# Block copies of the up-projection issued from SyncE's queue behind a semaphore, instead of from ScalarE's queue

## The chip, the cores and the metric

The kernel runs on one core of a Trainium2 chip. The metric is the device time of one execution in microseconds (us). A core has five engines, each with an instruction stream of its own that it works off in order: TensorE (PE in the profile), VectorE (DVE), ScalarE (ACT), GpSimd (POOL) and SyncE (SP). Engines wait for each other through semaphores, and an instruction that waits holds back all that stand behind it in its stream. A transfer (DMA) is issued by an instruction in one of these streams and then runs beside them.

## What is computed

Two layers of a bidirectional encoder over 1024 tokens of width 1024. The parts that matter here:

```python
def block_attention(q, k, v, scale):      # two groups of 6 heads in each layer
        s = jnp.einsum('bqhgd,bkhd->bhgqk', qi, k, preferred_element_type=jnp.float32) * scale
        p = jax.nn.softmax(s, axis=-1).astype(v.dtype)
        return jnp.einsum('bhgqk,bkhe->bqhge', p, v)
...
def conv_gated_ffn(h, w_up, conv_w, conv_b, w_down):
    a = h @ w_up
```

After the two attention groups come an output projection (`w_out`), a cross-attention to 256 memory tokens, and the gated FFN, whose product with `w_up` is done with seven block products instead of eight (the blocks are numbered m = 1 to 7). For four of the seven (m = 5, 6, 7, 3) sums of blocks of `w_up` are needed.

## The kernel before, in words

**Attention.** `attention()` walks over 24 items in each layer (12 heads, two halves of 512 queries), four steps `g` to an item. A step issues, in this order of the code: the scores of 128 queries (`score`: PE writes a `pair`, a PSUM tile of 128x1024, of which there are two; DVE takes the row maximum, line 292), the scaling of the step before (`scale`: a reciprocal on DVE, line 301, and a multiplication on POOL, line 302), two groups of four transposes of the item before (`turn`: PE line 137 into a `bank`, a PSUM tile of 128x512, of which there are four), the exponential (`expo`: ACT line 296), the products with the values (`value`: PE lines 315 and 316, one step late), and some side work (`fill`). Each transposed bank is split in two parts by `split`: ACT copies the high part (line 120, or 123 with a scale), then DVE subtracts it for the low part (line 121, or 124). Only when DVE has done so is the bank free for another group of transposes.

**Block sums.** During the attention the sums of `w_up` blocks are made by transfers from device memory to device memory: `up_copy` copies a piece (up to 1 MB), and four items later `up_add`, issued by POOL (line 781), adds another piece onto it. In each layer there are 24 copies and 24 additions. `extra` says at which item each is issued; all are issued in the step with `s == 2`. The sums are read in the FFN, after the attention.

**Order.** The code is not written to be run in this order word for word: the framework (`tile`) sorts each engine's stream by itself, by its own idea of what is ready when, and keeps only data dependences and what is pinned. `tc.keep_in_program_order` pins an instruction behind the one last written for the same engine. So a change in one stream can change the order in others.

**SP's queue.** SP issues the loads. During the attention it issued none between the loads of `w_uq` and `w_ukv` ahead of it and the eight loads of `w_out` towards its end (line 103, in `load`); POOL makes the high part of a loaded weight (line 107) and DVE the low part (line 108). Lines 693 and 694 (`y_split`) are a split of a finished output, done on POOL and DVE.

Of the kernel before, what the change touches and what calls it, by code (L numbers as in the profile page):

```python
# [11 lines left out]
ALU = mybir.AluOpType  # L12
# [57 lines left out]
def trunk(ctx: ExitStack, tc: tile.TileContext, a: dict, out: bass.AP):  # L70
    nc = tc.nc
# [8 lines left out]

    def f(ap):
        return ap.bitcast(F32) if ap.dtype == F32R else ap

    def stat():
        return stats.tile([P, 16], F32, tag="stat", name="stat")
# [14 lines left out]
    def load(src, cols, act=False):  # L100

        raw, hi, lo = sl.get(F32), sl.get(), sl.get()
        nc.sync.dma_start(raw[:, :cols], src)
        if act:
            nc.scalar.activation(hi[:, :cols], raw[:, :cols], AF.Copy)
        else:
            nc.gpsimd.tensor_scalar(hi[:, :cols], raw[:, :cols], 1.0, 0.0, ALU.mult, ALU.add)  # L107
        nc.vector.tensor_tensor(lo[:, :cols], raw[:, :cols], f(hi[:, :cols]), ALU.subtract)  # L108
        sl.put(raw)
        return hi, lo  # L110
# [6 lines left out]
    def split(src, hi, lo, scale=None):  # L117

        if scale is None:
            nc.scalar.activation(hi, src, AF.Copy)  # L120
            nc.vector.tensor_tensor(lo, src, f(hi), ALU.subtract)  # L121
        else:
            nc.scalar.activation(hi, src, AF.Copy, scale=scale)
            nc.vector.scalar_tensor_tensor(lo, src, scale, f(hi), ALU.mult, ALU.subtract)  # L124
# [115 lines left out]
    def head_norm(z, gain, tab):  # L240
# [29 lines left out]
        def turned():  # L270
# [3 lines left out]
            sl.put(*st["q"])  # L274

        return sums, scale, products, turned

    class Item:
# [20 lines left out]
        def scale(self, t):  # L299
            p, r = self.ps[t], stat()  # L300
            nc.vector.reciprocal(r[:, 0:1], self.den[:, t : t + 1])  # L301
            nc.gpsimd.tensor_scalar(p, p, r[:, 0:1], 0.0, ALU.mult, ALU.add)  # L302

        def turn(self, k):
            b = transpose4([p[:, k * P : (k + 1) * P] for p in self.ps])
# [85 lines left out]
    def layer(l, nt, last):  # L391
# [145 lines left out]
        for t in range(NT):  # L537
            b = proj(t, w_a, 416, 2)
            c, tt = divmod(t, TPC)
# [16 lines left out]
            if tt == TPC - 1:  # L556
                v, r = stat(), stat()
# [214 lines left out]
        up_sum = {(m, i): dpool.tile([P, n * CH + 16], F32, tag=f"u{l}_{m}_{i}", name=f"u{l}_{m}_{i}")[:, : n * CH] for m in (5, 6, 7, 3) for i, n in enumerate(UP_PARTS)}  # L772

        def up_piece(b, i):
            return a["w_up"][l, b][:, up_at[i] * CH : (up_at[i] + UP_PARTS[i]) * CH]

        def up_copy(m, i):
            tc.keep_in_program_order(nc.scalar.dma_start(up_sum[m, i], up_piece({5: 2, 6: 0, 7: 0, 3: 1}[m], i)))

        def up_add(m, i):  # L780
            tc.keep_in_program_order(nc.gpsimd.dma_start(up_sum[m, i], {5: lambda: up_piece(3, i), 6: lambda: up_sum[5, i], 7: lambda: up_piece(2, i), 3: lambda: up_sum[6, i]}[m](), accum_op=ALU.add))
# [61 lines left out]
        for n, (m, i) in enumerate(up_steps):  # L843
            extra.setdefault(n * 5 // 6, []).append(lambda m=m, i=i: up_copy(m, i))
            extra.setdefault(n * 5 // 6 + 4, []).append(lambda m=m, i=i: up_add(m, i))
# [537 lines left out]
```

## Time and profile before

| what | value |
|---|---|
| device time, median of 3 runs | 2869.32 us (2869.23 to 2872.6) |
| device time of the profiled execution | 2875.77 us |
| its span in the trace | 2873.6 us |
| PE busy | 97% of the span |
| DVE busy | 69% |
| ACT busy | 47% |
| POOL busy | 23% |

The busy shares are means over stages that differ: in the attention of the two layers (about 160 to 530 us and 1545 to 1960 us) DVE and ACT are far busier than in the FFN. An engine's idle time matters where the engine is the one that all wait for, here PE.

### The profile page before, as it was taken

How to read it: one execution, taken by the hardware profiler on the slowest of the kernel's cores; microseconds unless marked ns; L12 is line 12 of the kernel's file. 1: busy time of each engine (PE TensorE's matmuls, PEld its weight loads, DVE VectorE, ACT ScalarE, POOL GpSimd, SP SyncE). 2: the span in 40 equal slices, each digit the busy share in tenths (PEclk: the TensorE clock that was granted, in tenths of full speed). 3: DMA queues.
4: the chain of work that ended last, by engine and by line, in shares of the span. 5: the costliest groups of instructions: out<-in, count | busy, mean ns of one | idle time of the engine just before them, and what ended most of it. 6: DMA issues, size and time to landing. Idle time of an engine off the chain costs nothing. (4 is left out here: it accounts for less than half of the span.)

```text
span 2873.6 us, 37125 instructions
## 1 busy us (share of the span) xinstructions
PE 2798.3 (97%) x13909; PEld 2344.1 (82%) x13909; DVE 1975.6 (69%) x2825; ACT 1341.3 (47%) x2572; POOL 660.9 (23%) x628
## 2 busy tenths in 40 slices
PE   9998999999999999999999989999999999999998
PEld 7987787788878888888889777878887888888887
DVE  5578888656687777864445788895667877778544
ACT  4377877224554444310133778772345544443101
POOL 3244566320000000210123345663200000002100
PEclk9999999999999999999999999999999999999999
DMA  4015676311133333531110157752221333335311
GB/s 145 23 51 131 170 176 133 88 61 64 45 110 132 122 121 131 183 133 51 38 46 23 60 135 178 175 130 66 68 65 45 125 122 122 131 126 189 110 59 59
DMA packets 93635, 297.61 MB, mean 104 GB/s; under 512 B 10384, under 2 KB 11024, under 8 KB 83216
## 3 DMA queue, kind: packets, MB, share of 16 engines
q1 hardware_dynamic: 79488, 202.70, 21.1%
q0 software_dynamic: 6912, 46.14, 8.8%
q10 hardware_dynamic: 7056, 46.40, 4.5%
q8 instruction: 110, 1.80, 0.2%
q14 instruction: 69, 0.57, 0.1%
HBM read 267.94 MB, written 119.54 MB: 135 GB/s over the span
## 5 line engine op out<-in xcount | busy, mean ns | idle before, releaser
L113 PE MATMUL bank<-s,s 128*128 128x512 f32 (+4 forms) x1831 | 678.8, 371 | 5.9 <-DVE s L124 2.6
L115 PE MATMUL bank<-s,s 128*128 128x512 f32 (+4 forms) x1831 | 676.1, 369 | 0.9 <-DVE s L124 0.5
L114 PE MATMUL bank<-s,s 128*128 128x512 f32 (+4 forms) x1831 | 674.3, 368 | 0.0
L107 POOL TENSOR_SCALAR s<-s 128x1024 fp32r<-128x1024 f32 (+1 forms) x114 | 142.8, 1257 | 1374.3 <-DMA s<-in_w_down 1007.7
L121 DVE TENSOR_TENSOR s<-bank,s 128x512 fp32r<-128x512 f32 (+3 forms) x552 | 332.7, 631 | 109.1 <-ACT s L120 106.8
L120 ACT ACTIVATE s<-bank 128x512 fp32r<-128x512 f32 (+3 forms) x552 | 288.3, 555 | 238.4 <-PE bank L137 165.8
L113 PEld LDWEIGHTS bank<-s,s 128*128 128x128 f32 x1831 | 345.5, 189 | 62.7 <-DVE s L121 3.7
L115 PEld LDWEIGHTS bank<-s,s 128*128 128x128 f32 x1831 | 346.2, 189 | 53.8 <-DVE s L124 1.6
L114 PEld LDWEIGHTS bank<-s,s 128*128 128x128 f32 x1831 | 346.3, 189 | 50.9
L137 PE MATMUL bank<-ident,s 128*128 128x128 f32 (+1 forms) x2320 | 327.8, 276 | 45.5 <-DVE s L121 37.0
L137 PEld LDWEIGHTS bank<-ident,s 128*128 128x128 f32 (+1 forms) x2320 | 271.6, 141 | 108.0 <-issue 32.6
L302 POOL TENSOR_SCALAR s<-s,stat 128x1024 f32<-128x1024 f32 x192 | 224.5, 1169 | 249.1 <-DVE stat L301 159.6
L366 DVE TENSOR_TENSOR x<-x,bank 128x512 f32<-128x512 f32 x214 | 145.6, 683 | 195.5 <-PE bank L115 195.1
L292 DVE TENSOR_REDUCE stat<-pair 128x1 f32<-128x1024 f32 x192 | 234.2, 1220 | 65.4 <-PE pair L734 38.0
L1105 PE MATMUL bank<-s,s 128*128 128x512 f32 x704 | 274.8, 390 | 0.9 <-DVE s L206 0.9
L1106 PE MATMUL bank<-s,s 128*128 128x512 f32 x704 | 274.2, 389 | 0.0
L1104 PE MATMUL bank<-s,s 128*128 128x512 f32 x704 | 274.0, 390 | 0.0
L1057 ACT ACTIVATE s<-s 128x512 fp32r<-128x512 f32 x308 | 187.9, 627 | 161.7 <-PE bank L1106 49.8
L108 DVE TENSOR_TENSOR s<-s,s 128x1024 fp32r<-128x1024 f32 (+4 forms) x172 | 217.4, 1274 | 59.8 <-POOL s L107 46.1
L296 ACT ACTIVATE s<-pair,stat 128x1024 f32<-128x1024 f32 x192 | 214.3, 1116 | 16.9 <-DVE stat L292 10.3
L1058 DVE TENSOR_TENSOR s<-s,s 128x512 fp32r<-128x512 f32 x308 | 201.3, 687 | 24.4 <-ACT s L1057 20.8
L1104 PE MATMUL pair<-s,s 128*128 128x512 f32 x528 | 208.5, 395 | 1.2 <-ACT s L208 1.0
(164 smaller groups left out, 4519.5 us busy)
## 6 DMA issues: line engine op xcount, KB each, us to landing
s<-u SPq DMA_DIRECT2D x176, 256.0 KB, 3.0
u<-in_w_up ACTq DMA_DIRECT2D x40, 1024.0 KB, 6.5
s<-in_w_up SPq DMA_DIRECT2D x132, 256.0 KB, 3.3
g<-s SPq DMA_DIRECT2D x44, 512.0 KB, 2.8
s<-in_w_down SPq DMA_DIRECT2D x44, 512.0 KB, 4.4
s<-g SPq DMA_DIRECT2D x44, 512.0 KB, 5.4
u<-in_w_up POOLq DMA_DIRECT2D x20, 1024.0 KB, 9.8
u<-u POOLq DMA_DIRECT2D x20, 1024.0 KB, 10.0
```

The lines of the kernel that those rows point to most:

```text
L108: nc.vector.tensor_tensor(lo[:, :cols], raw[:, :cols], f(hi[:, :cols]), ALU.subtract)
L113: nc.tensor.matmul(o, l[0], r[0], start=first, stop=False)
L114: nc.tensor.matmul(o, l[0], r[1], start=False, stop=False)
L115: nc.tensor.matmul(o, l[1], r[0], start=False, stop=last)
L120: nc.scalar.activation(hi, src, AF.Copy)
L121: nc.vector.tensor_tensor(lo, src, f(hi), ALU.subtract)
L137: nc.tensor.transpose(b[:m, j * P : (j + 1) * P], s, ident)
L292: nc.vector.reduce_max(self.nm[:, 0:1], s, axis=AX.X, negate=True)
L302: nc.gpsimd.tensor_scalar(p, p, r[:, 0:1], 0.0, ALU.mult, ALU.add)
L1104: nc.tensor.matmul(o, lh, rh, start=k == 0 and m in (1, 5, 6), stop=False, skip_group_check=True)
L1105: nc.tensor.matmul(o, lh, rl, start=False, stop=False, skip_group_check=True)
L1106: nc.tensor.matmul(o, ll, rh, start=False, stop=k == 3, skip_group_check=True)
```

## The change

The copies are issued by SP instead of ACT, and are no longer pinned. Each waits by a semaphore for the POOL scaling (line 302) that was last written in the code when the copy is; `Item.last` remembers it. In a step with `s == 2` that is the scaling of the same item's second step.

```diff
@@ -80,6 +80,9 @@
+    def ins_of(i):
+        return getattr(i, 'ins', i)
...
@@ -299,7 +302,7 @@
         def scale(self, t):
             p, r = self.ps[t], stat()
             nc.vector.reciprocal(r[:, 0:1], self.den[:, t : t + 1])
-            nc.gpsimd.tensor_scalar(p, p, r[:, 0:1], 0.0, ALU.mult, ALU.add)
+            Item.last = nc.gpsimd.tensor_scalar(p, p, r[:, 0:1], 0.0, ALU.mult, ALU.add)
...
@@ -775,7 +778,8 @@
         def up_copy(m, i):
-            tc.keep_in_program_order(nc.scalar.dma_start(up_sum[m, i], up_piece({5: 2, 6: 0, 7: 0, 3: 1}[m], i)))
+            c = nc.sync.dma_start(up_sum[m, i], up_piece({5: 2, 6: 0, 7: 0, 3: 1}[m], i))
+            tc.add_manual_dep(ins_of(c), ins_of(Item.last).name, mybir.DependencyInfo(mybir.DependencyClass.Sync, mybir.DependencyReason.DATA), reason="not sooner")
```

No other instruction is added or taken away. Outside the attention the streams of PE, DVE, ACT and POOL stand in the same order as before; within it all four are sorted anew in places. In the rows that follow, line numbers of the changed kernel are 3 higher than those of the kernel before (L295 is L292, L304 is L301, L124 is L121, L106 is L103), and the copies are its line 781.

On DVE, at the turn from the fourth to the fifth item of the first layer (`s_187`, `s_188` are the two parts of transposed probabilities that are split, `stat<-pair` is the row maximum of a step's scores). Before:

```order
L292 TENSOR_REDUCE stat<-pair 128x1
L301 RECIPROCAL stat<-stat 128x1
L292 TENSOR_REDUCE stat<-pair 128x1
L121 TENSOR_TENSOR s_187_2299<-bank,s_187_2299 128x512
L121 TENSOR_TENSOR s_188_2307<-bank,s_188_2307 128x512
L301 RECIPROCAL stat<-stat 128x1
L121 TENSOR_TENSOR s_190_2332<-bank,s_190_2332 128x512
```

With the change, at the same place:

```order
L295 TENSOR_REDUCE stat<-pair 128x1
L304 RECIPROCAL stat<-stat 128x1
L124 TENSOR_TENSOR s_187_2299<-bank,s_187_2299 128x512
L124 TENSOR_TENSOR s_188_2307<-bank,s_188_2307 128x512
L295 TENSOR_REDUCE stat<-pair 128x1
L304 RECIPROCAL stat<-stat 128x1
L124 TENSOR_TENSOR s_190_2332<-bank,s_190_2332 128x512
```

The two splits of `s_187` and `s_188` have moved ahead of the second row maximum. PE's stream at this place is the same before and after.

On DVE again, at the start of the ninth item of the first layer, where a rotation of queries (lines 233 to 238, on `s_254` and `s_138`) lies between. Before:

```order
L301 RECIPROCAL stat<-stat 128x1
L233 TENSOR_TENSOR s_254_3007<-s_138_1673,s_73_703 128x128
L235 TENSOR_TENSOR s_254_3007<-s_138_1673,s_73_703 128x128
L292 TENSOR_REDUCE stat<-pair 128x1
L237 TENSOR_TENSOR s_138_1673<-s_254_3007 128x8x16
L238 TENSOR_TENSOR s_138_1673<-s_254_3007 128x8x16
L121 TENSOR_TENSOR s_248_2950<-bank,s_248_2950 128x512
L121 TENSOR_TENSOR s_249_2958<-bank,s_249_2958 128x512
```

With the change:

```order
L304 RECIPROCAL stat<-stat 128x1
L124 TENSOR_TENSOR s_248_2950<-bank,s_248_2950 128x512
L236 TENSOR_TENSOR s_254_3007<-s_138_1673,s_73_703 128x128
L124 TENSOR_TENSOR s_249_2958<-bank,s_249_2958 128x512
L124 TENSOR_TENSOR s_247_2925<-bank,s_246_2924 32x512
L295 TENSOR_REDUCE stat<-pair 128x1
```

The splits of `s_248` and `s_249` stood behind four products of the rotation and a maximum; now one such product stands ahead of the second.

On SP, towards the end of the first layer's attention (`u_7_5` is a sum that a copy begins, `s_527` a raw load of `w_out`). Before:

```order
L103 DMA s_123_1596<-in_w_uq 128x576
L103 DMA s_129_1608<-in_w_ukv 128x768
L103 DMA s_126_1602<-in_w_uq 128x576
L103 DMA s_527_5701<-in_w_out 128x1024
L103 DMA s_539_5850<-in_w_out 128x1024
```

With the change:

```order
L781 DMA u_6_5_1632<-in_w_up 128x2048
L781 DMA u_7_5_1638<-in_w_up 128x2048
L781 DMA u_3_4_1643<-in_w_up 128x2048
L781 DMA u_3_5_1644<-in_w_up 128x2048
L106 DMA s_527_5701<-in_w_out 128x1024
L106 DMA s_539_5850<-in_w_out 128x1024
```

All 24 copies of a layer now stand one behind the other on SP, between the load of `w_uq` and the first load of `w_out`.

## Rows read from the trace of the kernel before

**Rows 1.** The page, busy time and share of each engine.
```profile
PE 2798.3 (97%) x13909; PEld 2344.1 (82%) x13909; DVE 1975.6 (69%) x2825; ACT 1341.3 (47%) x2572; POOL 660.9 (23%) x628
```

**Rows 2.** Busy time in stretches: start:end, length, then PE, PEld, DVE, ACT, POOL.
```profile
160.00:530.00 370.00, 343.94 (x1934) 283.66 (x1933) 308.70 (x512) 290.41 (x597) 199.20 (x187) 0.99 0.54 135
...
205.00:455.00 250.00, 232.13 (x1299) 190.00 (x1298) 209.28 (x365) 203.26 (x404) 139.98 (x133) 0.99 0.64 158
455.00:520.00 65.00, 60.59 (x341) 49.29 (x340) 62.07 (x89) 46.54 (x84) 43.84 (x41) 1.00 0.51 115
1545.00:1960.00 415.00, 390.03 (x2180) 328.72 (x2179) 341.22 (x549) 307.46 (x661) 224.12 (x198) 0.98 0.50 122
```

**Rows 3.** PE's waits, first row of 160 to 530 us, then of 1545 to 1960 us.
```profile
PE bank L137 <- DVE s L121: 18.6, 18, 2.5
...
PE bank L137 <- DVE s L121: 18.4, 18, 2.6
```

**Rows 4.** Timeline, all engines, some rows, end of the fourth item of layer one.
```profile
221.38 0.50 ACTq L778 DMA_DIRECT2D u<-in_w_up  x1
221.58 1.13 POOL L302 TENSOR_SCALAR s<-s,stat 128x1024 f32<-128x1024 f32 x1
...
222.65 1.09 ACT L120 ACTIVATE s<-bank 128x512 fp32r<-128x512 f32 x2
...
224.92 1.22 DVE L292 TENSOR_REDUCE stat<-pair 128x1 f32<-128x1024 f32 x1 [1.12 <-PE pair L734]
...
226.06 1.28 DVE L121 TENSOR_TENSOR s<-bank,s 128x512 fp32r<-128x512 f32 x2
226.89 0.63 PE L137 MATMUL bank<-ident,s 128*128 128x128 f32 x4 [1.33 <-DVE s L121]
```

**Rows 5.** Timeline of PE in the first layer's attention, other rows with such idle time.
```profile
213.14 0.63 PE L137 MATMUL bank<-ident,s 128*128 128x128 f32 x4 [0.79 <-DVE s L121]
...
240.38 1.32 PE L137 MATMUL bank<-ident,s 128*128 128x128 f32 x8 [1.29 <-DVE s L121]
...
284.32 1.08 PE L137 MATMUL bank<-ident,s 128*128 128x128 f32 x4 [2.54 <-DVE s L121]
...
338.65 0.63 PE L137 MATMUL bank<-ident,s 128*128 128x128 f32 x4 [1.42 <-DVE s L121]
...
367.31 0.63 PE L137 MATMUL bank<-ident,s 128*128 128x128 f32 x4 [1.76 <-DVE s L121]
...
443.51 0.63 PE L137 MATMUL bank<-ident,s 128*128 128x128 f32 x4 [1.34 <-DVE s L121]
...
458.70 0.63 PE L137 MATMUL bank<-ident,s 128*128 128x128 f32 x4 [0.88 <-DVE s L121]
463.15 0.66 PE L137 MATMUL bank<-ident,s 128*128 128x128 f32 x4 [1.10 <-DVE s L121]
```

**Rows 6.** Timeline of PE, first two items: scores that waited for ACT.
```profile
169.51 0.50 PE L733 MATMUL pair<-s,s 128*128 128x512 f32 x1 [1.84 <-ACT s L296]
...
183.20 0.50 PE L733 MATMUL pair<-s,s 128*128 128x512 f32 x1 [0.76 <-ACT s L296]
```

**Rows 7.** Instructions on the block sums: duration in ns (least/median/most), first and last start.
```profile
L778 ACTq DMA_DIRECT2D u<-in_w_up x48: 497/498/635, 177.2 to 1878.2; - x48
L781 POOL DMA_DIRECT2D u<-in_w_up x24: 789/832/1171, 236.4 to 1902.0; - x24
```

**Rows 8.** The page, issues of transfers: count, size, median us to landing.
```profile
u<-in_w_up ACTq DMA_DIRECT2D x40, 1024.0 KB, 6.5
...
s<-in_w_out SPq DMA_DIRECT2D x16, 512.0 KB, 3.7
```

**Rows 9.** Timeline around the first load of `w_out`: SP, then POOL.
```profile
453.58 0.33 SPq L103 DMA_DIRECT2D s<-in_w_out  x1
...
460.48 1.48 POOL L107 TENSOR_SCALAR s<-s 128x1024 fp32r<-128x1024 f32 x1
465.13 1.13 POOL L302 TENSOR_SCALAR s<-s,stat 128x1024 f32<-128x1024 f32 x1 [3.17 <-DVE stat L301]
```

## The prediction, as it was made before the changed kernel ran

> **What bounds the kernel now.** I read the page first: PE is busy for 97% of the span [rows 1], so what can be won is PE's idle time, some 75 us, unless work is taken from PE, and this change takes none. The busy times by stretch say where the idle time lies: of 370 us of the first layer's attention PE is idle for 26, and of 415 us around the second's for 25 [rows 2]. That is two thirds of it, and the change touches these two stages alone. PE's waits in them, sorted by who ended them, have one large row: transposes (L137) that waited for DVE's low part of a split (L121), 18 times and 18.6 us in the first layer, 18.4 us in the second [rows 3]. A transpose needs a free bank, there are four, and a bank is free when DVE has made its low part. So in the attention PE waits for banks, and the question is why DVE frees them late.
>
> The timeline around one such wait answers it [rows 4]. ACT had both high parts done by 222.65 + 1.09 = 223.74 us. DVE stood idle for 1.12 us before 224.92, because the next instruction in its stream was the row maximum (L292) of scores that PE was still making, and took the splits only at 226.06. PE, next in line for that bank, stood still for 1.33 us until 226.89. The splits were ready and stood in DVE's stream behind an instruction that was not. The order before shows it: two row maxima with no split between them.
>
> How often? I went through DVE's order of before for row maxima with no full-width split (128x512) since the one before. Leaving the first item of a layer out, in which no transposes are due yet, and one place near the end, there are ten in each layer, each at the first step of an item. Their PE waits are the 1.33 us shown [rows 4], three more of exactly 1.33 (at 254.98, 298.81 and 311.20 us), and 0.79, 1.29, 1.42, 1.76, 1.34 and 0.88 [rows 5]: 12.80 us. Two waits have close relatives as their cause: 2.54 us at 284.32, where four rotation products and a maximum stand ahead of the splits (the second place of the order that is shown), and 1.10 at 463.15, where two splits of finished outputs (L694) stand ahead of one [rows 5]. Together 16.44 us in a layer, nearly all of the 18.6.
>
> **The change, part by part.**
>
> *ACT loses 24 issues in each layer*, 0.498 us each [rows 7], 12 us of its stream. ACT is busy for 290 of 370 us there [rows 2] and the issues run beside its work: the one at 221.38 stood in the way of nothing that PE then waited for [rows 4]. From below this is worth 0, from above all of 2 x 12 = 24 us. PE's list of waits is headed by DVE, not ACT, so I take 0.
>
> *SP gains them, each behind a wait for a POOL scaling.* Behind a waiting copy stand only the other copies and then the loads of `w_out`. The copy of 221.38 would go out when the scaling of 221.58 ends, at 222.71 [rows 4], 1.3 us later; its addition on POOL comes four items on (the first copy at 177.2, the first addition at 236.4 [rows 7]), and a copy lands in 6.5 us [rows 8]. Cost 0, with some 50 us of cover. At the end the first load of `w_out`, now at 453.58, stands right behind the last copy of 1 MB on the same queue. If it had to wait for the whole copy, it would land at 453.58 + 6.5 + 3.7 = 463.8 [rows 8, 9] instead of before POOL's use of it at 460.48. POOL would be 3.3 us late, and it is idle for 3.17 us ahead of its next scaling [rows 9]. So at worst a few tenths of POOL's time, with the rest of an item until PE needs that scaling: 0.
>
> *The streams are sorted anew.* This is the part that counts. In the changed order none of the ten places is left: the splits stand ahead of the maximum. Nor are the two others: at 284.32 one product stands ahead instead of four and a maximum, at 463.15 the second split comes ahead of both L694. What it is worth at the place shown: DVE would start the splits at 223.8 instead of 226.06 and be done with the first at about 224.5, and PE comes to its transposes at 226.89 - 1.33 = 225.56. No wait is left. The maximum behind the splits starts at 223.8 + 1.28 = 225.08 instead of 224.92, 0.16 late, with an item's lag until PE transposes what follows from it. A wait of PE that goes is a gain of its whole length, as PE has hardly another.
>
> The sum. First layer 16.44 us. Second: same order, and its row is 18.4 against 18.6, so 16.44 x 18.4 / 18.6 = 16.3. Together 32.7.
> - Less the 1.10 us at 463.15 in both layers, 2.2: from 455 to 520 us DVE is busy for 62.07 of 65 us [rows 2], so that the two L694 only move and DVE is as late soon after.
> - Less new waits: at four places of a layer the new order puts a maximum ahead of splits that it stood behind (by the old order at about 216, 251, 448 and 450 us). From below nothing, from above 1.22 us each (the maximum's length [rows 4]), 9.8 in all. At one of the four I expect it: 2.4.
> - More: the 0.76 us at 183.20 [rows 6] in both layers. The scores that waited there now stand behind some 18 products of side work: 1.5.
> - Less a tenth of what is left for waits that come back because DVE, busy for 209 of 250 us between 205 and 455 [rows 2], has less slack once PE runs faster: 3.0. This is a choice; the bounds are 0 and, with half of the gain back, 15.
>
> 32.7 - 2.2 - 2.4 + 1.5 - 3.0 = 26.6 us. The profiled execution took 2875.77 us (span 2873.6 and 2.2 around it), so it would take 2849.2. The median of the runs is 6.4 lower, 2869.32; I take the same gain from it: **2842.7 us**. For this case alone the range goes from 2834 (all 32.7 + 1.5 and some tenths of ACT's) to 2854 (15 us).
>
> **The rivals.**
>
> *Only the place of issue changes, and the time does not.* The new order moves waits instead of removing them: PE gets its bank and then stands at the next thing. For it: DVE is at 84% between 205 and 455 us and ACT's share is little lower [rows 2]. Against it: the places where DVE stood idle with ready work behind are gone, and this time was lost to both engines. The time would be that of before, less at most some tenths: about 2868. The Trainium skill has a rule that speaks for this rival: its page "DMA: Bandwidth & Descriptors", section "Issuing engines are not separate DMA queues", says that transfers run on the same 16 DMA engines whoever starts them, and that another issuer saves only the sequencer's time to start them. By that rule taken alone the gain lies between 0 and the 24 us of ACT's stream; the trace agrees in so far as the issues are short (0.498 us), and the rule is silent on the order of the other streams.
>
> *Half.* The ten waits shrink to some half, as splits that moved ahead are themselves held by ACT's high parts (line 120) at some places. For it: at 213.14 only 0.79 us were lost. Against it: at the place shown the splits had been ready for 2.3 us. Gain 6 to 15 us: about 2859.
>
> *Slower: scores run out of buffers.* PE's scores go to two `pair` tiles, and one is free when ACT's exponential has read it, which follows the maximum. With splits ahead of maxima the exponential is later, and PE then waits at its scores instead of its transposes. Such a wait cost 1.84 us at 169.51 [rows 6]. If it came at each of 24 items, 44 us in a layer, less 16.4 won: 2 x 28 = 55 us slower, 2924. It decides from 16.4 / 1.84 = 9 items of a layer. Against it: before, only the two waits of [rows 6] are of this kind, both in the first two items, and the maximum shown is only 0.16 us later.
>
> **How the numbers follow.** Chances: the forecast 0.68; half 0.12; no change 0.12; slower 0.05; more than 34 us 0.03. A measurement of this kernel can tell 0.2%, 5.7 us, from no change. Faster by more: 0.68 + 0.12 + 0.03 = 0.83; within: 0.12; slower: 0.05. The range must leave out no more than 2 in 10: from 2833 it goes up over the forecast's own range and most of the half case, to 2861. It leaves out no change, slower and more than forecast, 0.20.
>
> **What would show it.** In the changed profile PE's idle time in the first layer's attention should fall from 26 us to about 12, in the same row: L137 waiting for the low part should drop from 18 times and 18.6 us to some 3 us, with no wait over 1 us at the starts of items. DVE's rows before the maxima should show no idle time with splits behind. FFN, cross-attention and projections should have the same lengths. ACT should show no issues, and SP's copies should go out within 3 us of where ACT's did. If PE's waits on DVE are gone but new ones as long stand at scores (ended by ACT L296) or at values, the third or first rival holds. The prediction fails if the order of the streams that I read does not decide who waits, above all if splits that stand early in DVE's stream are not ready there.

## The result, and the profile after

The changed kernel takes 2837.33 us (median of four runs, 2835.61 to 2839.29) against 2869.28 for the kernel before, run beside it (2868.41 to 2872.6). The ratio is 0.9887, with a 95% interval from 0.9870 to 0.9904: faster by 32.0 us, where 26.6 were forecast. The two profiled executions are 40.2 us apart (2875.77 and 2835.61), since the one of before took longer than any of these four runs; the last section tells where the 8 us between the two differences lie. One run of e2_pin below (4595 us) and one of the kernel before, made beside e4, e5, e7 and e8 (4884 us), had a granted clock of TensorE under 0.6 of the full one, and the ratios leave them out.

The changed kernel's page, busy time and share of each engine, answers to [rows 1]:

```profile
PE 2787.6 (98%) x13909; PEld 2338.7 (83%) x13909; DVE 1968.5 (69%) x2825; ACT 1337.4 (47%) x2572; POOL 656.2 (23%) x628
```

Its busy times by stretch (start:end, length, then PE, PEld, which is PE's loading of weights, DVE, ACT, POOL; last the granted clock, the DMA engines' busy share, GB/s), the same stretches as in [rows 2]:

```profile
160.00:530.00 370.00, 359.46 (x2024) 297.04 (x2023) 317.13 (x526) 291.69 (x602) 206.08 (x193) 0.99 0.56 140
1545.00:1960.00 415.00, 404.03 (x2247) 337.43 (x2246) 344.25 (x559) 302.14 (x643) 226.74 (x204) 0.99 0.52 130
```

PE is idle for 370.0 - 359.5 = 10.5 us in the first layer's attention, where it was 26, and for 11 us around the second's, where it was 25. Little else moved: if each instruction of PE is set beside its namesake of before, the changed kernel runs 0.2 us ahead at 160 us, 20.3 at 480, still 20.3 at 1545, 40.7 at 1900 and 39.8 at the end. Outside the attentions the lead drifts by less than 2 us. So the difference was made in the two attentions.

PE's waits in the changed kernel from 160 to 530 us, first rows, answering to [rows 3] (us in total, times, longest; L140 is L137, L124 is L121):

```profile
PE pair L736 <- ACT s L299: 2.9, 3, 1.8
PE bank L140 <- DVE s L124: 2.5, 6, 1.1
PE bank L140 <- POOL s L305: 2.1, 3, 1.5
```

18 waits for the low part with 18.6 us are now 6 with 2.5. The place of [rows 4] in the timeline of the changed kernel, POOL, SP, DVE and PE:

```profile
218.48 1.11 POOL L305 TENSOR_SCALAR s<-s,stat 128x1024 f32<-128x1024 f32 x1
...
219.62 0.49 SPq L781 DMA_DIRECT2D u<-in_w_up  x1
...
220.49 1.27 DVE L124 TENSOR_TENSOR s<-bank,s 128x512 fp32r<-128x512 f32 x2
...
221.54 0.48 PE L318 MATMUL bank<-s,s 128*128 128x512 f32 x1
...
221.68 1.21 DVE L295 TENSOR_REDUCE stat<-pair 128x1 f32<-128x1024 f32 x1
221.86 0.60 PE L140 MATMUL bank<-ident,s 128*128 128x128 f32 x4
```

DVE's two splits (220.49) now run ahead of the maximum (221.68), DVE has no idle time before either, and the transposes at 221.86, which waited 1.33 us before, follow the product before them by 0.32 us. The copy goes out at 219.62, just as the scaling it waits for ends (218.48 + 1.11 = 219.59). A copy of 1 MB lands in 8.4 us instead of 6.5 [rows 8]; its addition comes 50 us later, and nothing waited for it.

### The profile page after: what moved, and what is told of

It is laid out like the page before. It is cut to its first block, busy times and chain, and to the rows that moved or that the text cites. A ratio compares the mean times of both kernels' runs of the same rounds, so it can differ in the third digit from the quotient of the medians.

```text
span 2833.8 us, 37136 instructions
## 1 busy us (share of the span) xinstructions
PE 2787.6 (98%) x13909; PEld 2338.7 (83%) x13909; DVE 1968.5 (69%) x2825; ACT 1337.4 (47%) x2572; POOL 656.2 (23%) x628
## 4 chain that ended last, share of the span: by engine, by line
PE 85%; DVE 6%; ACT 4%; issue 2%; POOL 2%; DMA 1%; SPq 0%; POOLq 0%; DVEq 0%; ACTq 0%
PE bank L116 12%; PE bank L118 12%; PE bank L117 12%; PE bank L140 6%; PE bank L1109 5%; PE bank L1110 5%; PE bank L1108 5%; PE pair L1108 4%; PE pair L1109 4%; PE pair L1110 4%; PE pair L116 2%; PE pair L118 2%; PE pair L117 2%; PE bank L318 2%; PE bank L319 2%
## 5 line engine op out<-in xcount | busy, mean ns | idle before, releaser
L124 DVE TENSOR_TENSOR s<-bank,s 128x512 fp32r<-128x512 f32 (+3 forms) x552 | 331.0, 629 | 106.1 <-ACT s L123 104.1
L140 PE MATMUL bank<-ident,s 128*128 128x128 f32 (+1 forms) x2320 | 321.1, 275 | 15.2 <-DVE s L124 5.1
L140 PEld LDWEIGHTS bank<-ident,s 128*128 128x128 f32 (+1 forms) x2320 | 269.9, 140 | 71.3 <-DVE s L124 11.1
L305 POOL TENSOR_SCALAR s<-s,stat 128x1024 f32<-128x1024 f32 x192 | 224.9, 1172 | 221.5 <-DVE stat L304 154.0
L295 DVE TENSOR_REDUCE stat<-pair 128x1 f32<-128x1024 f32 x192 | 233.7, 1217 | 41.6 <-PE pair L737 21.0
L1062 DVE TENSOR_TENSOR s<-s,s 128x512 fp32r<-128x512 f32 x308 | 201.1, 686 | 24.1 <-ACT s L1061 20.5
L108 ACT ACTIVATE s<-s 128x1024 fp32r<-128x1024 f32 (+3 forms) x58 | 58.2, 1005 | 323.1 <-DMA s<-g 155.8
```

Source lines behind the costliest of these rows:

```text
L140: nc.tensor.transpose(b[:m, j * P : (j + 1) * P], s, ident)
L295: nc.vector.reduce_max(self.nm[:, 0:1], s, axis=AX.X, negate=True)
L305: Item.last = nc.gpsimd.tensor_scalar(p, p, r[:, 0:1], 0.0, ALU.mult, ALU.add)
```

## The experiments

Three theories stood against each other. *Order*: the gain came with the new order of the streams. *Issue*: it came with the 24 issues of 0.498 us that ACT lost in each layer. *Transfer*: it came with the queue or the moment at which the copies go out. Each ratio is to runs of the kernel before made beside it, whose median was 2871 to 2873 us.

| run | what it is | median us | ratio, 95% interval |
|---|---|---|---|
| e7_old_order | changed kernel, all four streams (PE, DVE, ACT, POOL) in the old order | 2869.78 | 0.9997 [0.9988, 1.0005] |
| e8_new_order | kernel before, all four streams in the new order | 2836.79 | 0.9884 [0.9869, 0.9900] |
| e6_small | changed kernel, 24 small issues on ACT in a layer | 2836.44 | 0.9876 [0.9862, 0.9890] |
| e3_sp_pin | copies on SP without the wait, pinned | 2839.36 | 0.9886 [0.9874, 0.9899] |
| e4_sp_free | copies on SP with neither wait nor pin | 2844.87 | 0.9914 [0.9900, 0.9928] |
| e5_act_wait | copies on ACT with the wait | 2882.55 | 1.0043 [1.0030, 1.0056] |
| e1_late | changed kernel, ten maxima put back ahead of splits | 2850.47 | 0.9925 [0.9913, 0.9936] |
| e2_pin | kernel before, maxima kept behind splits | 2864.16 | 0.9973 [0.9963, 0.9983] |
| e10_new_dve | changed kernel, new order on DVE alone | 2872.09 | 1.0008 [0.9999, 1.0017] |
| e12_dve_act | new order on DVE and ACT | 2858.21 | 0.9951 [0.9939, 0.9964] |
| e14_dve_act_pe | new order on DVE, ACT and PE | 2842.30 | 0.9900 [0.9885, 0.9915] |
| e11_old_second | old order in the second layer alone | 2852.12 | 0.9941 [0.9927, 0.9954] |

### Order or issue: both orders with both places of issue

Kernels e7, e8, e10, e11, e12 and e14 hold streams in a given order by a table of instruction names, read at the end of the program. Its edges fix the order within an engine and add no semaphore. In the rows of e7, e10, e12 and e14 line numbers are 4 higher than those of the kernel before (L141 is L137, L125 is L121, L300 is L296, L306 is L302).

```python
def keep_order(tc):
    at = {i.name: i for i in tc.nc.cur_bb.bb.instructions}
    for first, *steps in json.loads(zlib.decompress(base64.b85decode(ORDER))):
        name, last = first, at[f"I-{first}"]
        for s in steps:
            name += s
            i = at[f"I-{name}"]
            tc.add_manual_dep(i, last.name, mybir.DependencyInfo(mybir.DependencyClass.NoSync, mybir.DependencyReason.DATA), reason="order of a table")
            last = i
```

```diff
     with tile.TileContext(nc) as tc:
         trunk(tc, aps, out)
+        keep_order(tc)
```

**e7_old_order** is the changed kernel with the table of before. DVE, ACT and POOL then stand as before instruction by instruction, PE but for 24 places.

> The changed kernel (copies on SP, each with its wait; no issues on ACT), but with the streams of PE, DVE, ACT and POOL in the attention of both layers held in the order that they had before the change, instruction by instruction, by order edges that need no semaphore. Order theory: 2869 us as before the change, within 4 us, with the 18 waits for the low part back in each layer. Issue theory and transfer theory: 2837 us as with the change. A part of the gain here (say 2855 us) would be shared out by it: what is missing to 2869 belongs to the place of issue, the rest to the order.

Measured: 2869.78 us, ratio 0.9997. Its wait of PE (first row, 160 to 530 us) is that of before:

```profile
PE bank L141 <- DVE s L125: 18.1, 18, 2.5
```

**e8_new_order** is the kernel before, its copies still issued and pinned on ACT, with the table of the changed kernel.

> The counterpart: the kernel before the change, its copies issued by ACT and pinned there, with the four streams held in the order that they have with the change. Order theory: 2837 us, within 4 us, plus what the 24 x 0.498 us of issues in ACT's stream cost: by the small copies issued on ACT (2836 us, no loss) nothing. Issue theory and transfer theory: 2869 us. The run before, which only kept maxima behind splits (2864 us), left the rotation products ahead of splits; if this run too stays near 2864, DVE's order is not what gave the time.

Measured: 2836.79 us, ratio 0.9884, the changed kernel's. **e6_small** gives ACT its issues back in the changed kernel:

```diff
+        small = {(m, i): dpool.tile([P, P], F32, tag=f"w{l}_{m}_{i}", name=f"w{l}_{m}_{i}") for m in (5, 6, 7, 3) for i in range(len(UP_PARTS))}
...
+            tc.keep_in_program_order(nc.scalar.dma_start(small[m, i], a["ident"][:, :P]))
```

> The changed kernel, and beside each copy on SP a small one (64 KB, of a constant into a scratch tile of its own) that ACT issues, pinned in its stream. This gives ACT back its 24 issues in each layer and keeps the order of the streams nearly as in the changed kernel. Order theory: 2838 to 2843 us (24 x 0.498 us of ACT's stream in a layer, most of it beside other work). Issue theory: the gain goes, 2860 us or more.

Measured: 2836.44 us, a little under the 2838 to 2843 that were expected: the issues cost nothing that can be seen. The framework sorted e6 a little differently from the changed kernel (DVE's stream differs in 112 of 2825 places, PE's in 358 of 13909), so e8, which has the copies themselves on ACT in the new order, is the cleaner of the two. The four corners are plain: old order 2869 to 2873 us from either queue, new order 2836 to 2837 from either queue. What the diff does by itself, moving copies to SP behind a semaphore, is worth nothing that these runs can tell; the new order that came with it is worth all. The Trainium skill's rule that the prediction weighed (page "DMA: Bandwidth & Descriptors", section "Issuing engines are not separate DMA queues": another issuer saves only the time to start a transfer) agrees with e7 (0.9997), and was silent on what decided.

### What the wait and the queue are worth

**e3_sp_pin** takes the semaphore away and leaves the order of the other four streams as it is with the change:

```diff
-            c = nc.sync.dma_start(up_sum[m, i], up_piece({5: 2, 6: 0, 7: 0, 3: 1}[m], i))
-            tc.add_manual_dep(ins_of(c), ...)
+            tc.keep_in_program_order(nc.sync.dma_start(up_sum[m, i], up_piece({5: 2, 6: 0, 7: 0, 3: 1}[m], i)))
```

> The changed kernel without the semaphore: the copies stand on SP in the order of the code, and nothing holds them, so they may all go out in one stretch at the start of the attention. The order of PE, DVE, ACT and POOL is that of the changed kernel, row for row. Order theory: 2837 us, within 4 us. Transfer theory (it matters when the copies run): another time, slower if 24 MB of copies in one stretch get in the way of the loads of that time, by up to some 10 us in a layer.

Measured: 2839.36 us, 0.07% above the changed kernel, which is no difference that these runs can tell. SP sent 22 copies in one stretch of 46.5 us from 165.65 on, and a copy took 25.9 us to land instead of 8.4; nothing waited for them. **e4_sp_free** takes the pin away too:

```diff
+            nc.sync.dma_start(up_sum[m, i], up_piece({5: 2, 6: 0, 7: 0, 3: 1}[m], i))
```

> The changed kernel with its copies on SP, but with neither the wait nor a pin, so that the framework lets them float: they stand at the start of a layer, among the loads of its projections' weights, and those of layer two stand within layer one. The order of DVE in the attention is as free of early maxima as with the change. If it matters that the copies come not sooner: slower than 2837 us at the projections ahead of the attention, where PE would wait for loads behind up to 24 MB of copies (at the 46 MB and some 235 us that the copies of before took for both layers at 6.5 us a MB in a row, up to some 100 us). If only the order matters: 2837 us, within 6 us.

Measured: 2844.87 us, some 8 us slower than the change, far less than the bound of 100 us. The place is one load of `w_uq` at the start of the first layer's attention. ACT, SP and PE in the timeline of e4:

```profile
164.80 0.33 SPq L106 DMA_DIRECT2D s<-in_w_uq  x1
...
170.19 0.85 PE L118 MATMUL bank<-s,s 128*128 128x288 f32 x2 [2.98 <-DVE s L127]
175.95 1.42 ACT L108 ACTIVATE s<-s 128x576 fp32r<-128x576 f32 x2 [6.95 <-DMA s<-in_w_uq]
...
176.68 1.09 PE L116 MATMUL bank<-s,s 128*128 128x288 f32 x3 [4.92 <-ACT s L108]
```

The load issued at 164.80 stands behind five copies that went out from 150.07 on. It landed 11.1 us after its issue, where the changed kernel's load of this place took 2.7. It keeps ACT waiting 6.95 us, and PE stands still two times around it, for 2.98 + 4.92 = 7.9 us, where the changed kernel stands still for 1.84 + 0.40. Some 2 us more go right behind it: the granted clock had fallen to 0.50 (1.2 GHz) while PE stood still, and is still 0.50 from 176 to 182 us. So the wait "not sooner" is worth some 8 us against copies that float, and nothing against copies that are only pinned. **e5_act_wait** makes the other half of the diff, the wait on ACT:

```diff
+            c = nc.scalar.dma_start(up_sum[m, i], up_piece({5: 2, 6: 0, 7: 0, 3: 1}[m], i))
```

> The change's wait without its change of queue: ACT issues the copies, unpinned, each behind a semaphore wait for the same POOL scaling, so that what stands behind a copy on ACT waits as well. The framework sorts DVE about as badly as before the change. Order theory: 2869 us or slower, by up to 1.3 us at each of 24 copies of a layer where ACT has work behind the copy, 2869 to 2900 us. If the wait (the later copies) itself gave the time: under 2850 us.

Measured: 2882.55 us, 0.43% slower than before. The framework sorted DVE about as before (PE's waits on the low part: 16.9 us in 18 times), and the waits now stood in ACT's stream. How much of the 11.6 us is the one and how much the other was not taken apart. Together with e3, whose four streams are the changed kernel's row for row, this tells which half of the diff brought the new order: the copies' leaving ACT's stream for SP's, and not the wait.

### Whose order

The first two runs set out to show that DVE's order is enough, as the prediction had it. **e1_late** writes the two low parts behind the next item's first maximum at ten places of a layer, in the changed kernel:

```diff
+LATE = (3, 4, 5, 6, 9, 10, 12, 14, 19, 20)
...
             if g < n:
                 items[i].score(s)
+            while held:
+                held.popleft()(True)
...
-                items[j].turn(2 * q)
-                items[j].turn(2 * q + 1)
+                hold = held if s == 3 and i + 1 in LATE else None
+                items[j].turn(2 * q, hold)
+                items[j].turn(2 * q + 1, hold)
```

Where `hold` is given, `turn` puts its low part on that list instead of writing it, and the low part is written, pinned, behind the next maximum.

> The changed kernel, but at ten places of each layer (the start of items 3, 4, 5, 6, 9, 10, 12, 14, 19 and 20) the two low parts of the last step's transposes are put behind the next item's first row maximum again, as they stood before the change. The copies stay on SP with their wait, and ACT has no issues. Order theory (the time went with DVE's order): PE's waits on the low part come back, about one of 1.0 to 1.8 us at each place; 10 to 20 us in a layer, so 2857 to 2872 us. As the framework sorts the rest around the pinned maxima anew, some places may be milder than before the change; under 2850 the order theory explains less than half. Issue theory (the time went with the 24 x 0.498 us of issues that ACT no longer has in each layer): 2837 us as the changed kernel, within 6 us. Transfer theory (the copies now go out later, or from another queue, and that gave the time): 2837 us as well.

Measured: 2850.47 us, some 13 us lost for both layers, short of the 20 expected at least. PE's waits on these low parts came back only to 3.8 us in the first layer. **e2_pin** does the reverse in the kernel before: each maximum behind the last low part.

```diff
-            nc.vector.reduce_max(self.nm[:, 0:1], s, axis=AX.X, negate=True)
+            m = nc.vector.reduce_max(self.nm[:, 0:1], s, axis=AX.X, negate=True)
+            if Item.low is not None:
+                tc.add_manual_dep(m.ins, Item.low.ins.name, mybir.DependencyInfo(mybir.DependencyClass.NoSync, mybir.DependencyReason.DATA), reason="behind the splits")
...
-            split(b, self.pt[k][:, :512], self.pt[k][:, 512:])
+            Item.low = split(b, self.pt[k][:, :512], self.pt[k][:, 512:])
```

> The kernel before the change, with its copies on ACT and pinned as they were; the one edit is that each row maximum is kept behind the last low part written ahead of it, so that DVE's splits stand ahead of the maximum at all the ten places. It adds no semaphore. Order theory: 2837 us as the changed kernel, within 6 us, with PE's waits on the low part down from 18.6 to some 3 us in the first layer. Issue theory and transfer theory: 2869 us, as before the change, since ACT's issues and the copies are as they were.

Measured: 2864.16 us, about 8 of the 32 us that the change is worth: a clear miss. In the first layer PE's waits on the low part fell from 18.6 to 7.8 us, while those of its scores on ACT grew from 2.6 to 5.0. The long waits left on the low part are of another kind. DVE, POOL and PE in the timeline of e2 (L305 is L302 there, L304 is L301):

```profile
276.40 1.21 POOL L305 TENSOR_SCALAR s<-s,stat 128x1024 f32<-128x1024 f32 x1 [2.16 <-DVE stat L304]
277.58 0.45 POOL L234 TENSOR_TENSOR s<-s,s 128x128 f32<-128x128 f32 x1
...
278.07 0.54 DVE L237 TENSOR_TENSOR s<-s 128x128 f32<-128x128 f32 x1 [1.45 <-POOL s L234]
...
278.74 1.28 DVE L121 TENSOR_TENSOR s<-bank,s 128x512 fp32r<-128x512 f32 x2
279.47 0.66 PE L137 MATMUL bank<-ident,s 128*128 128x128 f32 x4 [2.29 <-DVE s L121]
```

Here a rotation product (L237) stands ahead of the splits on DVE and waits for POOL, which first did a scaling. Since the framework had sorted all streams anew in e1 and in e2, neither run says which stream mattered. The tables can: **e10_new_dve**, **e12_dve_act** and **e14_dve_act_pe** are the changed kernel with the new order on one, two and three engines, and the old on the rest.

> The changed kernel with DVE alone in the order that it has with the change; PE, ACT and POOL are held in the order of before the change. It tells whose order gave the time. If it is DVE's, as predicted from DVE's idle time with splits behind: 2837 to 2845 us, with PE's waits on the low part nearly gone. If the new order of PE, ACT or POOL did it: 2855 us or more. Between these: what is missing to 2870 is DVE's part.

> The changed kernel with DVE and ACT in the order that they have with the change; PE and POOL are held in the order of before. With DVE alone in the new order (2872 us) the long waits for DVE were gone from PE, but DVE waited 24.9 us for ACT's high parts in the first layer's attention instead of 12.8. Pair theory (DVE's early splits are worth something only if ACT makes the high parts in the same order): 2837 to 2848 us, with DVE's waits for high parts back near 13 us. If PE's order is what was missing: still over 2860 us.

> The changed kernel with DVE, ACT and PE in the order that they have with the change; POOL alone is held in the order of before (40 of its 584 instructions differ in place). Pair theory and PE's order: 2837 to 2842 us, as what is left to POOL are scalings that change places with products of the rotation. If POOL's order carries a part of the gain: more than 2845 us, with PE's waits ended by the scaling on POOL.

Measured: 2872.09, 2858.21 and 2842.30 us. The first is the time of before. The second lies between the two cases that were expected, and the third at the edge of the case in which POOL brings nothing. Waits of e10 from 160 to 530 us, PE's and then DVE's:

```profile
PE bank L141 <- DVE s L125: 5.7, 12, 1.1
PE bank L141 <- POOL s L306: 3.7, 3, 1.3
PE pair L737 <- ACT s L300: 3.5, 4, 1.8
PE bank L117 <- ACT s L328: 3.3, 2, 1.7
...
DVE s L125 <- ACT s L124: 24.9, 34, 1.7
```

The same row of DVE in e12, after PE's first two rows:

```profile
PE pair L737 <- ACT s L300: 6.0, 5, 1.8
PE bank L141 <- POOL s L306: 3.9, 4, 1.2
...
DVE s L125 <- ACT s L124: 17.9, 29, 1.6
```

In e14:

```profile
PE bank L141 <- DVE s L125: 3.6, 7, 1.1
...
DVE s L125 <- ACT s L124: 14.2, 30, 1.6
```

And in the changed kernel:

```profile
DVE s L124 <- ACT s L123: 12.8, 28, 1.6
```

With DVE's order alone all thirteen waits that the prediction names, but that at 183.20, are 0.00, and nothing is gained: DVE now stands at its early splits until ACT has made the high parts (24.9 us; 13.2 in e7, 12.8 in the changed kernel), and PE at ACT and POOL. One such wait of PE in e10, with the rows of DVE and POOL that lead to it:

```profile
286.72 0.68 DVE L125 TENSOR_TENSOR s<-bank,s 32x512 fp32r<-32x512 f32 x1 [0.27 <-ACT s L124]
...
288.69 0.16 DVE L305 RECIPROCAL stat<-stat 128x1 f32<-128x1 f32 x1
289.02 1.12 POOL L306 TENSOR_SCALAR s<-s,stat 128x1024 f32<-128x1024 f32 x1 [2.43 <-DVE stat L305]
290.20 0.77 PE L141 MATMUL bank<-ident,s 128*128 128x128 f32 x5 [1.31 <-POOL s L306]
```

The reciprocal stands on DVE behind splits and a maximum, POOL's scaling waits 2.43 us for it, and PE waits 1.31 us for the scaling. In this order of adding the streams, ACT brings 14 us and PE 16 more by the medians. The last 5 us fall to POOL, but the intervals of e14 (0.9885 to 0.9915) and of the changed kernel (0.9870 to 0.9904) overlap, so that POOL's part isn't certain. (These are steps of one chain; the same stream could be worth another sum in another order. The old DVE order with the other three new was not run, so no run shows how much of the gain needs DVE's order.)

**e11_old_second** puts all four old orders back in the second layer alone.

> The changed kernel with the order of before put back in the second layer's attention alone. The two layers have the same order and should each hold half of the gain: 2853 us (2837 + 16), within 3 us. By the idle time shown at the thirteen places of a layer alone (16.4 + 0.8, with nothing given back) it would be 2854; by the prediction's 13.3 us in a layer 2850. If the layers' gains aren't independent: nearer to 2837 or to 2870.

Measured: 2852.12 us: 15 us more than the change, 19 less than before. So the first layer's gain does not need the second's, and each layer has about half. No kernel of these beat the changed one by more than 0.2%.

## Why the prediction was right, and where it was not

**The place and its bound.** Right: PE's idle time in the attentions was the whole of it, and every other stage kept its length to within 2 us.

**The sum.** The forecast was 26.6 us and the gain 32.0. The term that was too small is the length of the waits: 16.44 + 0.76 us in a layer by the idle time shown. That row counts from the modelled end of the matmul before. PE in e7 (old order):

```profile
223.64 0.47 PE L319 MATMUL bank<-s,s 128*128 128x512 f32 x1
...
225.45 0.63 PE L141 MATMUL bank<-ident,s 128*128 128x128 f32 x4 [1.34 <-DVE s L125]
```

From start to start these are 1.81 us, with the change 221.86 - 221.54 = 0.32. The wait cost 1.49 us and is shown as 1.34. Over the thirteen places of a layer e7 has 22.7 us from start to start and the changed kernel 2.3: 20.5 us, where e7's rows show 16.9. The Trainium skill says why a reader should expect it: its page "Perfetto Trace Analysis", section "Tensor Engine Instruction (MATMUL, LD_WEIGHTS)", has the profiler compute a matmul's end from its size instead of seeing it; the trace agrees, with 0.48 us for a matmul that the next follows after 0.32.

**The deductions.** Their sum was about right (2.2 + 2.4 + 3.0 = 7.6 us), their places were not. By the two profiles of e7 and the changed kernel the gain is 32.7 us (spans of 2866.5 and 2833.8), so that 2 x 20.5 - 32.7 = 8.3 us were given back. That this is near 7.6 is luck. The 1.10 us at 463.15 were gained (PE's gap there is 0.00), against the deduction of 2.2. What came anew are eleven waits of 0.3 us or more that neither the profile of before nor that of e7 has, six in the first layer and five in the second. They are 7.2 us by the idle time shown, and 8.6 from start to start, about what was given back. Some of them, in the changed kernel:

```profile
266.71 0.50 PE L736 MATMUL pair<-s,s 128*128 128x512 f32 x1 [0.58 <-ACT s L299]
...
315.65 0.33 PE L140 MATMUL bank<-ident,s 128*128 128x128 f32 x1 [0.40 <-POOL s L305]
...
356.56 0.66 PE L140 MATMUL bank<-ident,s 128*128 128x128 f32 x4 [1.50 <-POOL s L305]
...
1762.74 0.77 PE L140 MATMUL bank<-ident,s 128*128 128x128 f32 x5 [1.80 <-POOL s L305]
```

The longest, one in each layer, and the one at 315.65 wait for a POOL scaling, which no term named; the others wait for ACT's exponential or DVE's low part. What is left about cancels: 2.4 and 1.4 us are lost at the ends of the two attentions, where the changed kernel's granted clock falls, and 1.8 us each are won behind them. The four places with a maximum put ahead of splits, priced at 2.4, do not appear among the waits.

**The cause.** Here a step of the argument fell: that the time was lost because DVE had a maximum ahead of splits, and would be won by turning these round. The observation was right, and its price too small by the term above; but e10 shows that DVE's order alone moves the waits to ACT's high parts and POOL's scalings. That is the outcome of the first rival, by the mechanism that *Half* names: splits that moved ahead are held by ACT's high parts. The forecast held because the other three streams were sorted anew with DVE's. The prediction had read DVE's order at every place and PE's only at two, and no place of ACT's or POOL's order. So far it held by luck.

**ACT's issues and SP's queue.** Both valued at 0: right (e6 and e8 for the issues, e3 for the queue). The first load of `w_out` came at 436.00 us, right behind the last copy. That is 17.6 us sooner than before, but PE's work there is some 18 us ahead too, so that the load came no sooner by the work.

**The rivals.** *Only the place of issue changes*: true of the issue itself (e7), and of DVE's order by itself (e10), not of the change. *Half*: no by the time; its mechanism is what e10 shows. *Scores run out of buffers*: PE's waits for a `pair` are 2.9 us in the first layer, as against 2.6 shown in e7; three, nowhere near nine items. In e12, where PE keeps its old order, they grow to 6.0, and in e14, which differs in PE's order, they are 2.8: the mechanism exists, and PE's new order is what keeps it small.

## What to carry to other kernels

When a framework sorts the streams, moving one transfer can be worth 1% by what the sorting does, and nothing by itself, as here: compare the orders first, and keep the good order by explicit edges so that the next edit doesn't lose it. An order was a joint property here: turning round one engine's stream where it visibly waits may only hand the wait to the engine that feeds it. A wait of PE is better priced from start to start of the matmuls around it than by the idle time shown.

## What the runs showed of the hardware that was not expected

Runs of one order differ by several us through TensorE's granted clock. The busy times of two stretches of 20 us in the kernel before (last columns: granted clock, DMA share, GB/s):

```profile
1590.00:1610.00 20.00, 16.97 (x88) 14.31 (x86) 13.23 (x22) 14.39 (x47) 7.92 (x7) 0.83 0.28 93
1710.00:1730.00 20.00, 17.51 (x94) 14.84 (x95) 15.89 (x28) 14.12 (x26) 10.54 (x11) 0.91 0.66 178
```

and in e7, which has the same order:

```profile
1590.00:1610.00 20.00, 17.56 (x106) 15.91 (x107) 13.24 (x23) 14.63 (x52) 6.35 (x6) 0.91 0.22 79
1710.00:1730.00 20.00, 18.48 (x107) 15.26 (x105) 16.07 (x27) 17.29 (x32) 14.58 (x15) 1.00 0.48 118
```

Around the two attentions (160 to 560 us and 1530 to 1930 us) the profiled execution of before has six such stretches under 0.99, that of e7 two, and the span of before is 7.1 us longer (2873.6 and 2866.5). In the five stretches where its clock is the lower of the two, PE of before falls behind its namesakes in e7 by 1.0 to 1.6 us each, 7.0 in all. This is most of the 8 us by which the two profiles of before and after overstate the gain. At one of four such places in the attentions of the changed kernel the clock fell to 0.50, the lower of the two levels (1.2 GHz), in the two us from 498 on, after PE had stood still for 0.59 and 1.06 us in the three us before.
